# The shared projections as seven half-size products instead of eight, in a gated-DeltaNet and attention trunk

## The chip, the cores and the metric

The kernel runs on one core of a Trainium2 chip. A core has TensorE (PE: matrix products and transposes), VectorE (DVE), ScalarE (ACT), GpSimd (POOL) and SyncE (SP), which here issues the DMAs. The metric is the device time of one launch in microseconds, lower is better.

## The reference

One sequence of 2048 tokens and width 1024 passes a gated-DeltaNet layer and then an attention layer. Between them lie four projections that read the same normed rows; they are what the change concerns:

```python
# h: (2048, 1024), after the DeltaNet layer
u = rms_norm(h, kv_norm)
k, v, f = split(u @ kv_w, [1024, 2048])          # kv_w: (1024, 1024 + 1024 + 8)
k = rms_norm(k.reshape(heads of 128), kv_k_norm)
c = cumsum(log_sigmoid(f + kv_forget_bias))
q, z = split(rms_norm(h, fox_pre_norm) @ fox_w_in, [1024])   # (1024, 2048)
q = rms_norm(q.reshape(heads of 128), fox_q_norm)
# per head: softmax(q k^T / sqrt(128) + c_i - c_j, causal) @ v, times silu(z), @ fox_w_out, rms_norm, + h
```

All of it is float32. The kernel keeps that precision by splitting each operand of a product into a high and a low part in the fast matrix format (the high part is a rounded copy, the low part the difference), and by making three matmuls of each product: high by high, high by low, low by high.

## The kernel before

The span has five stages: the DeltaNet layer (0 to about 1250 us: 128 projection passes by quarters of the tokens, woven with the delta rule), its output projection (to 1397), the shared projections (1400.75 to 2169.73), attention over 8 heads (to about 2690), and the last output projection.

**Shared projections** (`Shared`). Tokens are taken in two halves of 1024. `hprep` loads 128 rows of the DeltaNet layer's result (`ht`), scales them by 1/rms, transposes them by eight 128x128 blocks on TensorE and splits the transposes into `hh` and `hl`; for the first half this runs between the steps of the output projection, for the second after the first half. Then `run(half)` goes through 16 blocks of 256 columns (4 each of k, q, v, z). `wsplit` loads a block's weights (two DMAs of 512 KB), multiplies the norm's gain in and splits them: ACT writes the high part (L818), DVE the low part (L819). For each pair `tp` of token tiles, `mm3` (L130 to L132) is called for 2 tiles x 8 pieces of the contraction, that is 48 matmuls of 256 columns. Over 2 halves, 16 blocks and 4 pairs these are 6144 matmuls. The block with number FORGET carries the 8 forget-gate columns as well, so its 384 matmuls have 264 columns.

`finish` handles a pair after the next pair's products: for k and q, ACT squares and sums each head (L854), DVE scales the sums (L855), POOL takes the power -1/2 (L119), DVE multiplies from PSUM (L860), and TensorE transposes (L866) for the store to `kT_d` and `qT_d`. For v the block is copied, for z it becomes z(1 + tanh(z/2)), and both are stored.

The attention's tile pool is opened before the projections run, so the first head's K, Q and gate loads are queued among the projections' own.

**What sets the order.** The program is written in loops; a scheduler places each engine's instructions from the program's order, the waits and the free buffers. Each engine then executes its own list in order: an instruction that waits holds all behind it.

## Time and profile before

| | |
|---|---|
| median of 3 runs | 2910.54 us (2903.28 to 2915.01) |
| the profiled execution's own time | 2906.28 us |
| its span, first to last instruction | 2904.6 us |
| mean granted TensorE clock | 0.989 |
| PE / DVE / ACT / POOL busy, share of the span | 96% / 59% / 46% / 24% |
| shared projections, first to last matmul | 1400.75 to 2169.73 us |

A busy share is an average over stages with different limits, and TensorE's matmuls are pipelined: the distance from one matmul's start to the next one's is what a matmul costs when they follow each other, while the listed duration is longer. Idle time ahead of an instruction stands in brackets in a timeline, with what ended it.

### The profile page before, as it was taken

What the parts mean: (1) busy time and instruction counts of PE and PEld (TensorE: products, weight loads), DVE (VectorE), ACT (ScalarE), POOL (GpSimd) and SP (SyncE); (2) the same over time, 40 slices, a digit from 0 to 9 for tenths busy, and PEclk for the clock granted to TensorE, in tenths of its full rate; (3) what the DMA queues carried; (4) which work ended last, traced back from release to release, by engine and by line L of the source; (5) the groups of instructions that cost most, each with busy time, mean ns of one, the idle gap of its engine ahead of it and who ended that gap; (6) DMA issues with size and microseconds to landing.
All of it is one profiled execution on the core that took longest, in us unless ns stands there. A gap on an engine that the chain in (4) does not pass through costs nothing.

```text
span 2904.6 us, 50726 instructions
## 1 busy us (share of the span) xinstructions
PE 2795.3 (96%) x18406; PEld 2432.1 (84%) x18406; DVE 1717.4 (59%) x5060; ACT 1337.3 (46%) x3695; POOL 704.2 (24%) x712
## 2 busy tenths in 40 slices
PE   7889999999999999899999999999999999999998
PEld 6677788878887788778999999999998888888787
DVE  6776777777767776644333124332329888888422
ACT  5445544454444444434344223443227677676421
POOL 6544211121111111123211000110004444443322
PEclk9999999999999999999999999999999999999999
DMA  7656444444443443645222323223323323232443
GB/s 234 214 163 192 148 153 136 158 150 130 151 159 118 154 137 108 201 141 164 95 88 88 95 95 113 95 88 95 112 82 101 99 91 98 92 97 75 158 140 109
DMA packets 295505, 371.64 MB, mean 128 GB/s; under 512 B 68443, under 2 KB 216150, under 8 KB 294230
## 3 DMA queue, kind: packets, MB, share of 16 engines
q1 hardware_dynamic: 295088, 368.33, 39.4%
q8 instruction: 145, 2.38, 0.3%
q14 instruction: 106, 0.87, 0.1%
q10 hardware_dynamic: 166, 0.06, 0.0%
HBM read 263.40 MB, written 104.92 MB: 127 GB/s over the span
## 4 chain that ended last, share of the span: by engine, by line
PE 64%; DVE 16%; ACT 3%; issue 3%; DMA 2%; POOL 2%; DVEq 0%; POOLq 0%; ACTq 0%; SPq 0%
DVE acc_q L392 4%; PE pt L1129 4%; PE ppv L130 2%; PE ps L132 2%; PE ppq L130 2%; PE ppv L131 2%; PE ppv L132 2%; PE ppq L131 2%; PE ppq L132 2%; PE ppwf L130 2%; PE ppwf L131 2%; PE ppwf L132 2%; PE ppz L130 2%; PE ppz L131 2%; PE ppz L132 2%
## 5 line engine op out<-in xcount | busy, mean ns | idle before, releaser
L130 PE MATMUL pp_q<-xh_q,wh_q 128*128 128x512 f32 x768 | 325.5, 424 | 1.5 <-ACT acc_q L390 0.8
L132 PE MATMUL pp_q<-xh_q,wl_q 128*128 128x512 f32 x768 | 307.3, 400 | 0.0
L131 PE MATMUL pp_q<-xl_q,wh_q 128*128 128x512 f32 x768 | 305.4, 398 | 0.0
L392 DVE SCALAR_TENSOR_TENSOR acc_q<-cx_q,cols,acc_q 128x512 f32<-128x512 f32 x288 | 227.5, 790 | 12.9 <-ACT acc_q L390 9.7
L125 DVE TENSOR_TENSOR pl<-pt,ph 128x512 fp32r<-128x512 f32 (+1 forms) x320 | 192.1, 606 | 37.8 <-ACT ph L124 36.1
L124 ACT CAST ph<-pt 128x512 fp32r<-128x512 f32 (+1 forms) x320 | 161.7, 519 | 89.1 <-PE pt L1129 88.6
L395 ACT ACTIVATE th_q<-acc_q 128x512 f32<-128x512 f32 x96 | 60.8, 633 | 277.5 <-DVE acc_q L392 274.1
L1115 ACT ACTIVATE s<-s,nm 128x128 f32<-128x128 f32 (+15 forms) x128 | 154.5, 1207 | 68.3 <-DVE nm L1113 68.0
L1129 PE MATMUL pt<-ident,s 128*128 128x128 f32 x1088 | 172.1, 273 | 3.4 <-DVE pl L125 2.6
L132 PEld LDWEIGHTS pp_q<-xh_q,wl_q 128*128 128x128 f32 x768 | 145.6, 190 | 34.0
L130 PEld LDWEIGHTS pp_q<-xh_q,wh_q 128*128 128x128 f32 x768 | 146.1, 190 | 27.3 <-ACT acc_q L390 1.3
L131 PEld LDWEIGHTS pp_q<-xl_q,wh_q 128*128 128x128 f32 x768 | 146.0, 190 | 26.3 <-DVE xl_q L240 0.8
L1129 PEld LDWEIGHTS pt<-ident,s 128*128 128x128 f32 x1088 | 133.5, 140 | 33.6 <-DVE pl L125 3.7
L130 PE MATMUL ppk<-wh_k,hh 128*128 128x256 f32 x512 | 146.9, 287 | 2.6 <-issue 2.6
L130 PE MATMUL ppq<-wh_q,hh 128*128 128x256 f32 x512 | 146.8, 287 | 0.0
L130 PE MATMUL ppv<-wh_v,hh 128*128 128x256 f32 (+1 forms) x512 | 144.9, 283 | 0.0
L130 PE MATMUL ppz<-wh_z,hh 128*128 128x256 f32 x512 | 144.3, 282 | 0.0
L132 PE MATMUL ppv<-wh_v,hl 128*128 128x256 f32 (+1 forms) x512 | 143.9, 281 | 0.0
L131 PE MATMUL ppk<-wl_k,hh 128*128 128x256 f32 x512 | 143.9, 281 | 0.0
L131 PE MATMUL ppv<-wl_v,hh 128*128 128x256 f32 (+1 forms) x512 | 143.9, 281 | 0.0
L132 PE MATMUL ppk<-wh_k,hl 128*128 128x256 f32 x512 | 143.8, 281 | 0.0
L131 PE MATMUL ppq<-wl_q,hh 128*128 128x256 f32 x512 | 143.7, 281 | 0.0
(482 smaller groups left out, 8571.7 us busy)
## 6 DMA issues: line engine op xcount, KB each, us to landing
wh_q<-w_d SPq DMA_DIRECT2D x72, 512.0 KB, 3.5
wl_q<-w_d SPq DMA_DIRECT2D x72, 512.0 KB, 4.8
w_d<-wh_q SPq DMA_DIRECT2D x24, 512.0 KB, 4.4
w_d<-wl_q SPq DMA_DIRECT2D x24, 512.0 KB, 3.1
wh_q_z<-w_d SPq DMA_DIRECT2D x24, 512.0 KB, 3.3
wl_q_z<-w_d SPq DMA_DIRECT2D x24, 512.0 KB, 4.1
wr_q<-in_gdn_w_in_dram SPq DMA_DIRECT2D x22, 512.0 KB, 5.2
x_q<-in_x_dram SPq DMA_DIRECT2D x16, 512.0 KB, 4.5
```

The lines of the kernel that those rows point to most:

```text
L124: i = k.nc.scalar.copy(hi, src)
L125: (eng or k.nc.vector).tensor_tensor(out=lo, in0=src, in1=f(hi), op=ALU.subtract)
L130: nc.tensor.matmul(out, ah, bh, start=start, stop=False)
L131: nc.tensor.matmul(out, ah, bl, start=False, stop=False)
L132: nc.tensor.matmul(out, al, bh, start=False, stop=stop)
L392: nc.vector.scalar_tensor_tensor(out=acc, in0=cx[:, j:j + TB], scalar=cw[j], in1=acc, op0=ALU.mult, op1=ALU.add)
L395: nc.scalar.activation(th, acc, AF.Tanh, scale=0.5)
L1115: e = nc.scalar.activation(s[:, 0:w], s[:, 0:w], AF.Exp, bias=nm, accum_out=ls[:, ii:ii + 1])
L1129: nc.tensor.transpose(out=pt[:, ii * P:(ii + 1) * P], in_=Ps[ii][:, j * P:(j + 1) * P], identity=k.ident)
```

## The change

The product of 256 token rows by 512 columns over 1024 of contraction, which was 2 x 2 x 2 block products, becomes the Winograd form of Strassen's product: seven block products of (128 rows) x (512 of contraction) x (256 columns), of row sums and column sums.

- **Rows.** `prep` makes, for a pair of token tiles, the four quarters of the transposed rows, three further sums of them on POOL (four subtractions or additions of 128x512) and splits all seven operands. The row operands of three pairs at most are kept (`BLOCKS` of 2, 3 and 3 pairs).
- **Weights.** The gain is multiplied into all four 1024x1024 weights during the DeltaNet layer (`gain`: 32 times a load of 512 KB, a 128x1024 ACT instruction and a store of 512 KB to `wg_d`). For each of 24 groups (3 blocks of pairs x 8 groups of 512 columns, in the order k, k, q, q, v, v, z, z) `raw` loads 2 x 1 MB, `sums` makes four differences of 128x1024 on POOL, and `columns` splits the seven column operands (ACT the high part, DVE the low part, 128x1024 each).
- **Products.** Per group, product and pair 12 matmuls of 256 columns: 24 groups hold 64 pair-groups, 64 x 7 x 12 = 5376 matmuls.
- **Results.** A product is added up in PSUM with others where the form allows it and then taken out: two ACT copies and five DVE additions of 128x256 per pair-group.
- **k and q.** `finish` works on the 256x512 result in SBUF: ACT squares 128x1024, DVE sums per head (`tensor_reduce`), POOL takes the power (128x8), DVE multiplies 128x1024 with the result, and eight transposes follow on TensorE 5 and 6 ticks later (a tick is one pair of one product).
- **Forget gate.** `forget` makes 32 matmuls of 128 columns per pair and two small transposes.
- **Attention's pool** is opened after the projections have closed theirs.

```diff
+    def gain():
+        count[0] += 1
+        if count[0] % 3 or not gained:
+            return
+        i, kt = gained.pop(0)
+        wn, base, col = (("kv_w", 0, C_KVN), ("fox_w_in", 0, C_FPN), ("kv_w", D, C_KVN), ("fox_w_in", D, C_FPN))[i]
+        w = ins[wn] if wn == "kv_w" else ins[wn][0]
+        wr = p2.tile([P, D], F32, tag="x", bufs=4, name=f"wgr{i}_{kt}")
+        nc.sync.dma_start(wr, w[kt * P:(kt + 1) * P, base:base + D])
+        nc.scalar.activation(wr, wr, AF.Copy, scale=k.cols[:, col + kt:col + kt + 1])
+        nc.sync.dma_start(wg_d[i, kt], wr)
...
+        s1 = p2.tile([P, 4, P], F32, tag="s1", name=f"s1_{p}")
+        both(s1, q[1, 0], q[1, 1], ALU.add)
+        parts(q[0, 0], "P1")
+        yield
+        both(q[1, 0], q[0, 0], q[1, 0], ALU.subtract)
+        both(q[0, 0], s1, q[0, 0], ALU.subtract)
+        parts(q[0, 0], "P6")
...
+        for i, terms in enumerate(((("P1", 0), ("P2", 4)), (("P5", 0), ("P4", 8)))):
+            for j, (name, w0) in enumerate(terms):
+                for kt in range(4):
+                    for n, part in enumerate(self.rows[name, slot]):
+                        nc.tensor.matmul(pf[:, i], self.wf[:, w0 + kt], part[:, kt], start=i + j + kt + n == 0,
...
+    def sums(self, g, i):
+
+        lo, hi = self.quads[g, 0], self.quads[g, 1]
+        T = self.quads
+        a, b = {1: (lo[:, :, 1], lo[:, :, 0]), 2: (hi[:, :, 1], T.get((g, "T1"))), 3: (hi[:, :, 1], lo[:, :, 1]),
+                4: (hi[:, :, 0], T.get((g, "T2")))}[i]
+        t = T[g, f"T{i}"] = T[g, "T2"] if i == 4 else self.tt.tile([P, 4, 256], F32, tag=f"T{i}", name=f"T{g}_{i}")
+        self.k.nc.gpsimd.tensor_tensor(out=t, in0=a, in1=b, op=ALU.subtract)
...
+        self.raw(0)
+        for i in (1, 2, 3):
+            self.sums(0, i)
+        for n in range(ahead):
+            ready.append(self.columns(*work[n]))
...
+            if pi == 0:
+                cc, one, X, Y = {}, {}, {}, {}
+                if g + 1 < NG:
+                    self.raw(g + 1)
+                self.sums(g, 4)
+            if g + 1 < NG and pi in (2, 4, 5):
+                self.sums(g + 1, {2: 1, 4: 2, 5: 3}[pi])
+            if n + ahead < len(work):
+                ready.append(self.columns(*work[n + ahead]))
+            bh, bl = ready.pop(0)
...
+                    for j, (a, w) in enumerate(((ah, bh), (ah, bl), (al, bh))):
+                        nc.tensor.matmul(R, a[:, kt], w[:, kt], start=first and kt + j == 0,
+                                         stop=last and kt + j == 5, skip_group_check=True)
...
+                if name != "P1":
+                    c = cc[p]
+                    c11, c12, c21, c22 = (c[:, i, j * 256:j * 256 + 256] for i in range(2) for j in range(2))
...
+                    nc.scalar.copy(one[p], R)
+                elif name == "P2":
+                    nc.scalar.copy(c11, R)
...
+                    dst, src = {"P6": (c12, one[p]), "P7": (c21, c12), "P5": (c22, c21), "P4": (c21, c12), "P3": (c12, c12)}[name]
+                    nc.vector.tensor_tensor(out=dst, in0=src, in1=R, op=ALU.add)
+                if name == "P3":
+                    self.finish(g, p, c, pend)
+                tick()
...
+            sq = self.q1.tile([P, 8, P], F32, tag="sq", name="sq" + n)
+            nc.scalar.activation(sq, c8, AF.Square)
+            ss = q2.tile([P, 8], F32, tag="kss", name="kss" + n)
+            nc.vector.tensor_reduce(out=ss, in_=sq, axis=mybir.AxisListType.X, op=ALU.add)
+            nc.vector.tensor_scalar(out=ss, in0=ss, scalar1=1.0 / P, scalar2=EPS, op0=ALU.mult, op1=ALU.add)
+            rs = q2.tile([P, 8], F32, tag="krs", name="krs" + n)
+            rsqrt(k, rs, ss, 8)
+            nc.vector.tensor_tensor(out=c8, in0=c8, in1=rs.unsqueeze(2).to_broadcast([P, 8, P]), op=ALU.mult)
...
+                for i in range(4):
+                    h, t = i // 2, i % 2
+                    nc.tensor.transpose(out=pt[:, i], in_=c8[:, 4 * t + 2 * hh + h], identity=k.ident)
...
+            pend.append([5, lambda: turn(0)])
+            pend.append([6, lambda: turn(1)])
...
-    at = Attention(k, ar)
...
+    sh.run(h_d)
     sb.close()
     sa.close()
+    at = Attention(k, ar)
```

(In the first lines of `run`, `PRODUCTS` is the order P1, P6, P7, P5, P2, P4, P3, and operands are split two products ahead.)

**Order on VectorE in a k column block, before.** `kssk`, `knk` and `ppk` carry block and pair in their names; `wl` is the low part of the next block's weights. L860 reads PSUM.

```order
L860 TENSOR_SCALAR knk2_0_16200<-ppk2_0_16063,krsk2_0_16198 128x128 x4
L819 SCALAR_TENSOR_TENSOR wl_k3_0_16360<-wr_k3_0_1_16371,cols_87,wh_k3_0_16359 128x256 x4
L855 TENSOR_SCALAR kssk2_1_16260<-kssk2_1_16260 128x4
L860 TENSOR_SCALAR knk2_1_16272<-ppk2_1_16139,krsk2_1_16270 128x128 x4
L855 TENSOR_SCALAR kssk2_2_16336<-kssk2_2_16336 128x4
L860 TENSOR_SCALAR knk2_2_16348<-ppk2_2_16211,krsk2_2_16346 128x128 x4
L855 TENSOR_SCALAR kssk2_3_16430<-kssk2_3_16430 128x4
L860 TENSOR_SCALAR knk2_3_16442<-ppk2_3_16287,krsk2_3_16440 128x128 x4
```

The four scalings of a pair follow its own sums, and its transposes come after the next pair's products.

**Order on VectorE after, where a q group (10, pairs 2 to 4) ends and a v group (11) begins.** `gl11_P7` is the low part of a column operand of group 11, `cc10_2` the 256x512 result of pair 2, `kss` its sums and `krs` their power; L989 takes a product out of PSUM.

```order
L1037 TENSOR_REDUCE kss10_2_19143<-sq10_2_19141 128x8
L989 TENSOR_TENSOR cc10_4_18921<-cc10_4_18921,Y10_4_18977 128x256
L1038 TENSOR_SCALAR kss10_2_19143<-kss10_2_19143 128x8
L125 TENSOR_TENSOR gl11_P7_19197<-T11_3_19079,gh11_P7_19196 128x1024
L1041 TENSOR_TENSOR cc10_2_18861<-cc10_2_18861,krs10_2_19146 128x1024
L1037 TENSOR_REDUCE kss10_3_19164<-sq10_3_19162 128x8
L1038 TENSOR_SCALAR kss10_3_19164<-kss10_3_19164 128x8
L1041 TENSOR_TENSOR cc10_3_18891<-cc10_3_18891,krs10_3_19167 128x1024
L1037 TENSOR_REDUCE kss10_4_19185<-sq10_4_19183 128x8
L989 TENSOR_TENSOR cc11_2_19257<-one11_2_19201,X11_2_19200 128x256
L1038 TENSOR_SCALAR kss10_4_19185<-kss10_4_19185 128x8
L125 TENSOR_TENSOR gl11_P5_19254<-T11_1_18943,gh11_P5_19253 128x1024
```

Sums, power and product of three pairs now follow one another in one list with the splits of the next group's operands between them.

**Order on GpSimd at the same place, after.** `T11_2` to `T12_2` are the differences of weights for groups 11 and 12; before, this engine held only the powers here.

```order
L913 TENSOR_TENSOR T11_2_19034<-w11_1_18797,T11_2_19034 128x1024
L119 TENSOR_TENSOR krs10_2_19146<-kss10_2_19143,mhalf_76 128x8
L913 TENSOR_TENSOR T12_3_19475<-w12_1_19193,w12_0_19191 128x1024
L119 TENSOR_TENSOR krs10_3_19167<-kss10_3_19164,mhalf_76 128x8
L119 TENSOR_TENSOR krs10_4_19188<-kss10_4_19185,mhalf_76 128x8
L913 TENSOR_TENSOR T12_1_19339<-w12_0_19191 128x1024
L913 TENSOR_TENSOR T12_2_19430<-w12_1_19193,T12_1_19339 128x1024
```

A power (L119) now stands behind a difference of weights, and between two powers stands another.

**Order on SyncE before, where the projections end.** `vtz` are blocks of z, `kr`, `qr`, `vr` and `zr` loads for attention with the head's number.

```order
L889 DMA z_d_105<-vtz3_5_24425 128x2x256
L889 DMA z_d_105<-vtz3_6_24479 128x2x256
L889 DMA z_d_105<-vtz3_7_24484 128x2x256
L1006 DMA vr0_0_24679<-v_d_104 128x4x128
L1025 DMA qr0_3_24711<-qT_d_103 128x512
L1138 DMA zr0_0_24824<-z_d_105 128x4x128
L1138 DMA zr0_1_24860<-z_d_105 128x4x128
L1006 DMA vr0_1_24858<-v_d_104 128x4x128
L1004 DMA kr1_0_24874<-kT_d_102 128x512
```

Of head 0 only the last quarter of Q, V and z stand behind the last store; the other K and Q loads come earlier in the list.

**Order on SyncE after, at the same place.** `cc23` are the last three results of z.

```order
L1064 DMA z_d_106<-cc23_5_23955 128x2x512
L1064 DMA z_d_106<-cc23_6_23969 128x2x512
L1064 DMA z_d_106<-cc23_7_23983 128x2x512
L1187 DMA kr0_0_24254<-kT_d_103 128x512
L1187 DMA kr0_1_24260<-kT_d_103 128x512
L1187 DMA kr0_2_24266<-kT_d_103 128x512
L1187 DMA kr0_3_24272<-kT_d_103 128x512
L1321 DMA zr0_0_24562<-z_d_106 128x4x128
L1321 DMA zr0_1_24598<-z_d_106 128x4x128
L1208 DMA qr0_0_24278<-qT_d_104 128x512
L1208 DMA qr0_1_24297<-qT_d_104 128x512
```

All K and Q loads of head 0 now stand behind the last stores of z.

## Rows read from the trace of the kernel before

**Rows 1.** Busy by stretch: length, PE, PEld, DVE, ACT, POOL, granted clock, DMA share, GB/s.
```profile
300.00:1200.00 900.00, 876.47 (x5641) 717.19 (x5641) 657.41 (x2190) 426.71 (x1378) 135.72 (x112) 1.00 0.45 145
1200.00:1300.00 100.00, 87.76 (x515) 71.27 (x514) 53.93 (x161) 36.33 (x103) 29.93 (x30) 0.93 0.45 137
1400.00:1500.00 100.00, 98.75 (x833) 98.22 (x834) 35.20 (x114) 41.78 (x177) 18.38 (x18) 1.00 0.29 94
1900.00:2000.00 100.00, 100.00 (x851) 100.00 (x850) 32.22 (x107) 39.89 (x165) 15.12 (x15) 1.00 0.28 89
```

**Rows 2.** Groups of instructions on TensorE, 1400 to 2170 us.
```profile
L130 PE MATMUL ppk<-wh_k,hh 128*128 128x256 f32 x512 | 146.9, 287 | 2.6 <-issue 2.6
L130 PE MATMUL ppv<-wh_v,hh 128*128 128x264 f32 x128 | 36.3, 284 | 0.0
L866 PE MATMUL ptrk<-ident,knk 128*128 128x128 f32 x128 | 20.2, 276 | 0.5 <-DVE knk L860 0.5
```

**Rows 3.** Timeline of TensorE where the projections end: start, duration, instruction.
```profile
2165.84 0.28 PE L130 MATMUL ppz<-wh_z,hh 128*128 128x256 f32 x1
...
2169.73 0.22 PE L130 MATMUL ps<-kh,qh 128*128 128x128 f32 x1
2169.79 0.28 PE L131 MATMUL ps<-kl,qh 128*128 128x128 f32 x1
2169.90 0.27 PE L132 MATMUL ps<-kh,ql 128*128 128x128 f32 x1
2170.01 0.33 PE L130 MATMUL ps<-kh,qh 128*128 128x256 f32 x1
```

**Rows 4.** Timeline of TensorE where the projections begin.
```profile
1397.14 1.04 PE L790 MATMUL pth<-ident,ht 128*128 128x128 f32 x8
1400.75 0.36 PE L130 MATMUL ppk<-wh_k,hh 128*128 128x256 f32 x1 [2.58 <-issue]
```

**Rows 5.** Groups of instructions on VectorE, whole span.
```profile
L125 DVE TENSOR_TENSOR olwg<-orwg,ohwg 128x1024 fp32r<-128x1024 f32 x16 | 19.6, 1223 | 7.4 <-ACT ohwg L124 7.4
L785 DVE TENSOR_SCALAR ht<-ht,hrs 128x1024 f32<-128x1024 f32 x16 | 13.1, 818 | 19.1 <-DMA ht<-h_d 19.1
L437 DVE TENSOR_TENSOR attn_q0g<-pk_q,E_q 128x256 f32<-128x256 f32 x16 | 6.7, 417 | 0.0
```

**Rows 6.** Groups of instructions on GpSimd, whole span.
```profile
L119 POOL TENSOR_TENSOR rn_q<-ssn_q,mhalf 128x8 f32<-128x8 f32 x32 | 52.9, 1653 | 278.2 <-DVE ssn_q L417 275.8 <-DMA d_q0g<-Ti_q0g 2.1
L125 POOL TENSOR_TENSOR vl<-vr,vh 128x512 fp32r<-128x512 f32 x32 | 41.5, 1296 | 82.3 <-ACT vh L124 81.8
L1035 POOL TENSOR_TENSOR cd<-cb 128x1024 f32<-128x1024 f32 x7 | 13.3, 1896 | 39.2 <-DVE mx L1106 39.2
```

**Rows 7.** Groups of instructions on ScalarE, whole span.
```profile
L124 ACT CAST ohwg<-orwg 128x1024 fp32r<-128x1024 f32 x16 | 16.8, 1048 | 7.9 <-PE ppwg L131 7.9
L212 ACT ACTIVATE jx_q<-x_q 128x1024 bf16<-128x1024 f32 x16 | 16.9, 1057 | 8.4 <-DMA x_q<-in_x_dram 8.2
```

**Rows 8.** Timeline of VectorE, early in the projections and in attention.
```profile
1404.15 1.27 DVE L819 SCALAR_TENSOR_TENSOR wl_k<-wr_k,cols,wh_k 128x256 fp32r<-128x256 f32 x3
...
2223.95 0.69 DVE L125 TENSOR_TENSOR kl<-kr,kh 128x512 fp32r<-128x512 f32 x1
2225.37 2.43 DVE L125 TENSOR_TENSOR ql<-qr,qh 128x512 fp32r<-128x512 f32 x1
```

**Rows 9.** Timeline of GpSimd at the same places.
```profile
1400.02 2.52 POOL L722 TENSOR_TENSOR ywg<-ywg,xrwg 128x512 f32<-128x512 f32 x2 [0.92 <-DVE ywg L719]
1404.31 0.72 POOL L119 TENSOR_TENSOR hrs<-s1wg,mhalf 128x1 f32<-128x1 f32 x1 [1.77 <-DVE s1wg L729]
...
2223.99 3.25 POOL L1035 TENSOR_TENSOR cd<-cb 128x1536 f32<-128x1536 f32 x1
```

**Rows 10.** DMA issues: tensor, count, KB each, us to landing.
```profile
kr<-kT_d SPq DMA_DIRECT2D x32, 256.0 KB, 3.0
cb<-c_d SPq DMA_DIRECT2D x8, 1024.0 KB, 5.5
```

More of the change, by code (lines that the diff above doesn't have):

```diff
@@ L191, in gdn @@
     kept = []
+    gained = [(i, kt) for i in range(4) for kt in range(KT)]
+    count = [0]
+    def gain():
[9 more added lines that the diff above has]
+        nc.sync.dma_start(wg_d[i, kt], wr)
     turns, first = [], {}
@@ L313, in wsplit @@
                 nc.sync.dma_start(f(wl), w_d[ct, 1])
+                gain()
                 return wh, wl
@@ L795, in hprep, with parts @@
                 yield
-        self.hT[tb] = (hh, hl)
-    KINDS = (("k", "kv_w", 0, C_KVN), ("q", "fox_w_in", 0, C_FPN), ("v", "kv_w", D, C_KVN), ("z", "fox_w_in", D, C_FPN))
-    def wsplit(self, i, half):
+        pool = self.a2 if slot == 2 else self.a1
+        def parts(src, name):
+            hi = pool.tile([P, 4, P], F32R, tag=f"h{name}_{slot}", name=f"h{name}_{p}")
+            lo = pool.tile([P, 4, P], F32R, tag=f"l{name}_{slot}", name=f"l{name}_{p}")
+            split(k, hi, lo, src)
+            self.rows[name, slot] = hi, lo
@@ new lines, in both @@
+        def both(out, a, b, op):
+            nc.gpsimd.tensor_tensor(out=out, in0=a, in1=b, op=op)
+        s1 = p2.tile([P, 4, P], F32, tag="s1", name=f"s1_{p}")
[5 more added lines that the diff above has]
+        parts(q[0, 0], "P6")
+        yield
+        parts(q[1, 0], "P7")
+        yield
+        parts(s1, "P5")
+        yield
+        parts(q[0, 1], "P2")
@@ L802, in wsplit, with forget_weights @@
+        yield
+        parts(q[1, 1], "P4")
+        yield
+        both(q[0, 1], q[0, 1], q[0, 0], ALU.subtract)
+        parts(q[0, 1], "P3")
+        yield
+    def forget_weights(self):
         k = self.k
         nc = k.nc
-        kind, wn, base, gcol = self.KINDS[i // 4]
-        w = self.ins[wn] if wn == "kv_w" else self.ins[wn][0]
-        col = base + (i % 4) * 256
-        nm = f"{kind}{i % 4}_{half}"
-        pool = (self.p1, self.q1)[i % 2] if i else self.p1
-        n = 256 + (H if i == FORGET else 0)
@@ new lines, in forget_weights @@
+        for kt in range(KT):
+            nc.vector.tensor_scalar(out=wr[:, kt], in0=wr[:, kt], scalar1=k.cols[:, C_KVN + kt:C_KVN + kt + 1],
+                                    scalar2=None, op0=ALU.mult)
+        nc.vector.tensor_tensor(out=wr[:, KT:12], in0=wr[:, 4:KT], in1=wr[:, 0:4], op=ALU.subtract)
+        nc.scalar.copy(self.wf[:, :, 0:H], wr)
+        nc.vector.tensor_tensor(out=self.wf[:, :, H:2 * H], in0=wr, in1=f(self.wf[:, :, 0:H]), op=ALU.subtract)
+        self.t = self.q1.tile([P, L // P, H], F32, name="ft")
@@ L824, in run @@
+    def run(self, h_d):
         k, q2 = self.k, self.q2
         nc = k.nc
[L826 to L898 removed]
@@ L899, in run, with tick @@
-        last[0](*last[1:])
+        NG = 8 * len(self.BLOCKS)
+        work = [(g, name) for g in range(NG) for name in PRODUCTS]
+        ready = []
+        ahead = 2
+        pend = []
+        def tick():
+            for e in list(pend):
+                e[0] -= 1
+                if e[0] < 0:
+                    pend.remove(e)
+                    e[1]()
+        self.raw(0)
[3 more added lines that the diff above has]
+            ready.append(self.columns(*work[n]))
@@ L1234, in tile_yoco @@
     chain.close()
-    sh = Shared(k, ins, dram, sa)
-    halves = (x for tb in range(2) for x in sh.hprep(tb, h_d))
-    ready = [2 * KT * (i + H_LAG) + j * KT for i in range(8) for j in range(2)]
+    sh = Shared(k, ins, dram, wg_d, sa)
+    parts = (x for p, slot in sh.BLOCKS[0] for x in sh.prep(p, slot, h_d))
+    ready = [2 * KT * (i + H_LAG) + j * KT for i in range(4) for j in range(2)]
+    ready = ready[0:4] + [ready[3] + 8 + 2 * i for i in range(7)] + ready[4:8] + [ready[7] + 8 + 2 * i for i in range(7)]
     for _ in steps:
@@ L1242, in tile_yoco @@
             ready.pop(0)
-            next(halves)
-    for _ in halves:
+            next(parts)
+    for _ in parts:
         pass
-    first = sh.wsplit(0, 0)
     wo.close()
-    at = Attention(k, ar)
     sh.open2(sb)
-    sh.run(0, first)
-    first = sh.wsplit(0, 1)
-    for tb in (2, 3):
-        for _ in sh.hprep(tb, h_d):
-            pass
-    sh.run(1, first)
+    sh.run(h_d)
     sb.close()
     sa.close()
+    at = Attention(k, ar)
     w2 = []
```

276 lines of the change are left out of this document (163 added, 113 removed).

## The prediction, made before the changed kernel ran

> **What bounds the kernel now.** I read the busy shares of the span first, then the stretches, then TensorE's timeline at both ends of the shared projections, and last the durations of the operations that the change uses more of. In the stretches [rows 1] the reader is to see that TensorE is occupied 98.75 and 100 of 100 us in the projections at a granted clock of 1.00, while VectorE is at 32 to 35, ScalarE at 40 to 42 and GpSimd at 15 to 18. So this stage is bound by matmuls. A matmul of 256 columns costs its distance to the next: 33 from 2165.84 to 2169.73 are 0.118 us each; one of 128 columns costs 0.11 (2169.79 to 2169.90 to 2170.01) [rows 3]. The stage lasts 769.0 us, from 1400.75 [rows 4] to 2169.73 [rows 3]. Its content is 6144 x 0.118 = 725.0 (twelve groups of 512 and the like [rows 2]), 1.4 for eight more columns in 384 of them (0.118 x 8/256 each), and 256 + 64 transposes at 0.11 = 35.2, together 761.6. The other 7.4 us are waits.
>
> **What goes and what comes on TensorE.** 768 matmuls go: -90.6, and the eight columns: -1.4. The forget gate comes back as 256 matmuls of 128 columns: +28.2. (They are small, but TensorE pays almost as much for 128 columns as for 256.) The 256 transposes of k and q stay; 32 transposes of rows move from the output projection, where TensorE is just as full, into this stage: nothing. So the work falls by 63.8, and since I count the new kernel's waits one by one, I take off the old 7.4 too: -71.
>
> **What the other engines get.** Per group seven low parts of 128x1024 on VectorE, 1.22 each [rows 5]: 8.5 us; five additions of 128x256 from PSUM per pair, 0.42 each [rows 5]; for k and q a sum and a product of 128x1024 per pair. The product has two SBUF inputs like the low part: 1.2. The sum has no like in the trace: between 0.82 (one-input operation of that size) and 1.22 [rows 5]; I take 1.1, since it must read each element and accumulate. On GpSimd four differences of 128x1024 per group: between 1.90 and 2 x 1.30 = 2.6 [rows 6]; I take 2.4, nearer to the two-input subtraction. With three pairs a group has 252 matmuls or 29.7 us, with two pairs 19.8. VectorE needs 8.5 + 6.3 + 6.9 = 21.7 in a k or q group of three pairs, GpSimd 9.6 + 3 x 1.65 = 14.6. By sums it fits. Two things make it not fit by order.
>
> First, the two engines exclude each other. VectorE's low part of 128x512, from SBUF, takes 0.69 at 2223.95; at 2225.37 the same operation takes 2.43, and ends at 2227.80, 0.56 after GpSimd's 128x1536 that began at 2223.99 and ran 3.25 [rows 8, 9]. So it waited for all of it. The Trainium skill (SBUF — State Buffer, Who interferes with whom) says that a VectorE instruction with two SBUF inputs and a GpSimd instruction that reads SBUF take a shared port in turn, and whichever comes first keeps it; the trace agrees with the 2.43. By that rule GpSimd's power would hold the port as well. The row does not bear this out for a short one: at 1404.31 a power of 0.72 runs beside three low parts that take 1.27 together, as they do alone [rows 8, 9]. By the rule 32 powers of 1.65 would delay operand splits by up to 53 us of VectorE, most of it where VectorE waits for them anyway; the sum below has none of it.
>
> Second, the end of a k or q group is a chain. In its order above, VectorE's list is sum, (split), product, sum, product, sum, split, product, so each pair's power on GpSimd lies between two VectorE instructions of which the later one blocks the next pair: sum 1.1 + power 1.65 [rows 6] + product 1.2 + two or three handovers of some 0.1 = 4.2 us per pair. TensorE comes for a pair every 12 matmuls and 8 transposes, 1.4 + 0.9 = 2.3 us.
>
> **Step through a three-pair group,** from the end of the first pair's last product. Addition 0.4, ACT's square 1.06 [rows 7], sum 1.1, scaling 0.1, handovers: the power starts at 3.2 and ends at 4.85. Then GpSimd starts the next difference at once and holds it to 7.3; the product waits for it and ends at 8.5 to 9. TensorE wants the transposes after five pair-products, 5 x 12 x 0.118 = 7.1. The second pair: sum, then its power, product done at about 13, wanted at 11.3 with the first delay counted; the third, behind an operand split, at 17 to 20, wanted at 15.6 to 16.4. Together 3.7 to 7.4, I take 5.3. Eight such groups: +42 (28 to 59). With two pairs the power stands behind a difference of 2.4; the product ends at 9.6, wanted at 6.85: 2.75 in each of four groups, +11 (8 to 14).
>
> **The row operands** of six pairs are made during groups of products: seven splits of 128x512 at 0.69 and four GpSimd operations at 1.30 are 10 us that exclude each other. A v or z group of three pairs has 29.7 - 8.5 - 9.6 = 11 us free of this, one of two pairs 2 us. Pairs 3 and 4 fall into groups of two pairs: I take +14 there and +6 for the others, +20 (0 to 40).
>
> **The start.** Now TensorE waits 2.58 between the last transposes and the first product [rows 4]. After the change the second half of the first weights is queued on SyncE behind the last rows of the output projection, which end at 1400.02 + 2.52 = 1402.5 on GpSimd [rows 9]. A store's issue and a load of 1 MB (5.5 [rows 10]) bring it to 1408.5; then the second difference, 2.4, and the split, 1.05 [rows 7] + 1.22. The second product starts at about 1413 and only 2 x 12 matmuls (2.8) lie ahead of it: +11 (8 to 16).
>
> **The end.** The first attention matmul now comes 0.12 behind the last one of z [rows 3], because head 0's K and Q were loaded earlier. In the new order they stand behind the last stores of z, which wait for the addition, the tanh and the product: 0.4 + 1.06 + 1.2; then a load lands in 3.0 [rows 10], and a cast (half of 1.05) and a split (0.69 [rows 8]) follow: 6.9. Ahead of the first Q are three stores of 512 KB and six loads of 256 KB, 3 MB in all: nothing if they overlap what waits, 16 us if they went one by one at 1 MB in 5.5 [rows 10]. I take 3: +10 (7 to 23).
>
> **The DeltaNet stage** gets 32 loads, ScalarE instructions of 1.06 and stores. TensorE is occupied 876 of 900 us there, DMA 0.45, ScalarE 427 [rows 1]. There is room for 34 us of ScalarE; but each instruction waits for a load issued just before it and holds the convolution's scalings behind it. I take +6; if each cost its own time it would be 34, so 0 to 35.
>
> **The clock.** In the stretch where TensorE is occupied 87.8 of 100 us the granted clock is 0.93, in the full ones 1.00 [rows 1]. The k and q groups would be 4 x 24.5 + 8 x 37.5 = 398 us at about 87%; if they fell alike, 398 x 0.87 x 0.06 = 21. Short gaps spread evenly may not do that: I take +5 (0 to 21).
>
> **The sum:** -71 + 42 + 11 + 20 + 11 + 10 + 6 + 5 = +34. On the profiled execution's 2906.3 that is 2940; the median of the runs is 4.2 above it, which I leave within the range. What this measurement can tell from no change is about 0.5%, 14.5 us, so 2925 and 2896 are the bounds.
>
> **Rivals.**
> A. The forecast, 2905 to 2970, chance 0.46.
> B. Some half of the waits: the differences of weights finish before the powers are due (GpSimd at 1.9 instead of 2.4) and the lower ends hold. Three-pair groups 24, two-pair groups 6, rows 8, ends 18, rest 4: +60 against -71, 2895. For it: by sums VectorE and GpSimd are free a third of the time. Against: the chain of 4.2 against 2.3 needs no GpSimd difference. Chance 0.20.
> C. The saving arrives: the products wait for nothing but the two ends (+21) and some 8 us: -42, 2864. For it: TensorE alone bounded the stage, and the transposes are put 5 and 6 pair-products late, so the first pair is nearly covered. Against: second and third pair. Chance 0.21, faster.
> D. Worse: the clock falls to 0.93 in k and q groups (21 instead of 5), the DeltaNet stage pays for each gain instruction (34 instead of 6): 2984. For it: the stretch at 87.8. Against: the load has a queue of its own in time, and ScalarE is half idle. Chance 0.13.
>
> Slower by over 0.5%: 0.41 of A and all of D, 0.54. Within 0.5%: 0.05 of A, 0.12 of B, 0.01 of C: 0.18. Faster: 0.08 of B and 0.20 of C: 0.28. The range reaches down into C and up to D: 2866 to 2986; the forecast's own is 2905 to 2970.
>
> **What would show it.** TensorE's timeline at the end of a k or q group: idle ahead of the transposes (L1049), released by VectorE's product (L1041), 2 to 3 us per pair with three pairs, or none (C). VectorE's L125 and L1041 with mean durations over 1.22 and a maximum near 2.4 to 3.6 show the exclusion; means of 1.2 refute it. The second product of the first group should start near 1413. The first attention matmul should be about 10 us behind the last product. The stretch 300 to 1200 should be longer by some us, or not. I am wrong above all if the products' own waits in the twelve v and z groups are larger than the chain, or if the chain is hidden.

## The result and the profile after

The changed kernel takes 3066.65 us (median of 4 runs, 3062.26 to 3070.30) against 2906.91 (4 runs); the ratio is 1.0546 (95% interval 1.0515 to 1.0577). The direction is the one forecast; the loss, some 160 us, is nearly five times the 34 forecast and lies outside the range. The profiled execution took 3070.3 us with a span of 3068.3 and a mean granted clock of 0.957.

The same stretches of time as in [rows 1], with two of the projections, columns as there:

```profile
300.00:1200.00 900.00, 868.46 (x5616) 709.95 (x5607) 648.34 (x2160) 449.74 (x1394) 134.95 (x112) 0.99 0.55 178
1200.00:1300.00 100.00, 92.89 (x534) 74.96 (x533) 55.34 (x174) 37.61 (x108) 25.79 (x26) 0.93 0.46 135
1700.00:1800.00 100.00, 87.51 (x646) 85.70 (x645) 52.24 (x71) 32.35 (x44) 31.20 (x14) 0.86 0.21 69
2200.00:2300.00 100.00, 98.17 (x809) 98.03 (x810) 56.53 (x104) 36.15 (x49) 24.38 (x11) 0.97 0.28 99
```

In 1700 to 1800 (k and q groups of three pairs) TensorE is occupied 87.5 of 100 us at a clock of 0.86, in 2200 to 2300 (mostly v and z groups) 98.2 at 0.97. The stage is not slow everywhere. Its ends, as in [rows 3, 4]:

```profile
1413.87 0.39 PE L132 MATMUL ppwg<-wgwh,olwg 128*128 128x512 f32 x1
1421.24 0.77 PE L978 MATMUL X<-gh_P,hP 128*128 128x256 f32 x2 [6.55 <-POOL hrs L119]
```

```profile
2316.99 0.28 PE L978 MATMUL Y<-gh_P,lP 128*128 128x256 f32 x1
2334.92 0.44 PE L130 MATMUL ps<-kh,qh 128*128 128x128 f32 x1 [17.65 <-ACT qh L124]
```

The last matmul of the output projection starts at 1413.87 instead of 1396.90 (+17.0), the last one of the projections 903.1 us later instead of 772.7 (+130.4), and the first one of attention 17.9 after that instead of 0.1 (+17.8). What follows is 1.5 shorter. Together 163.7, the whole difference of the spans.

Inside the stage, summed over TensorE's timeline from the first product to the last (895.7 us): 702 are the work at the distances of [rows 3], as worked out; 120 are idle time, 75 of it ahead of the transposes of k and q (L1049); 73 are matmuls at a wider distance. By groups, the twelve in which a finish of k or q falls (from the second k group of a block to its first v group) carry 140 of these 193 us, the very first group 13, the other eleven 41. One group's waits:

```profile
1799.80 0.28 PE L978 MATMUL Y<-gh_P,lP 128*128 128x256 f32 x1
...
1810.35 0.89 PE L1049 MATMUL ptr<-ident,cc 128*128 128x128 f32 x4 [3.18 <-DVE cc L1041]
1810.89 0.56 PE L978 MATMUL X<-gh_P,hP 128*128 128x256 f32 x1
1811.26 0.41 PE L978 MATMUL X<-gl_P,hP 128*128 128x256 f32 x1
...
1814.66 0.63 PE L1049 MATMUL ptr<-ident,cc 128*128 128x128 f32 x4 [0.26 <-DVE cc L1041]
...
1817.81 0.28 PE L978 MATMUL X<-gl_P,hP 128*128 128x256 f32 x1
1822.20 1.09 PE L1049 MATMUL ptr<-ident,cc 128*128 128x128 f32 x4 [4.12 <-DVE cc L1041]
```

The matmul at 1799.80 is the last of the first pair's products. Ahead of this pair's transposes TensorE waits 3.18 us for L1041, the product with the power; after that matmuls follow each other at 0.21 instead of 0.118 until the second pair's transposes begin; ahead of the third pair's it waits 4.12. Waits (7.6) and wider distances (4.6) together make the group 44.5 us long, where its work is 32.3. From 1822 to 1827 the granted clock is 0.50, which is the level of 1.2 GHz, and from 1830 on it is 1.00:

```profile
1822.00:1827.00 5.00, 4.80 (x23) 4.83 (x24) 2.03 (x4) 2.21 (x3) 0.00 (x0) 0.50 0.05 18
1830.00:1845.00 15.00, 15.00 (x129) 15.00 (x128) 7.02 (x11) 5.21 (x7) 2.41 (x1) 1.00 0.35 112
```

What VectorE and GpSimd do ahead of the first and the last of these waits:

```profile
1802.56 1.22 DVE L1037 TENSOR_REDUCE kss<-sq 128x8 f32<-128x1024 f32 x1 [0.61 <-ACT sq L1035]
1804.03 0.17 DVE L1038 TENSOR_SCALAR kss<-kss 128x8 f32<-128x8 f32 x1
1804.10 1.22 DVE L125 TENSOR_TENSOR gl_P<-T,gh_P 128x1024 fp32r<-128x1024 f32 x1
1806.85 3.36 DVE L1041 TENSOR_TENSOR cc<-cc,krs 128x1024 f32<-128x1024 f32 x1 [1.53 <-POOL krs L119]
...
1813.29 1.23 DVE L1041 TENSOR_TENSOR cc<-cc,krs 128x1024 f32<-128x1024 f32 x1 [1.75 <-POOL krs L119]
...
1815.96 1.22 DVE L125 TENSOR_TENSOR gl_P<-T,gh_P 128x1024 fp32r<-128x1024 f32 x1
1818.70 3.35 DVE L1041 TENSOR_TENSOR cc<-cc,krs 128x1024 f32<-128x1024 f32 x1 [1.53 <-POOL krs L119]
```

```profile
1801.12 2.41 POOL L913 TENSOR_TENSOR T<-w,T 128x1024 f32<-128x1024 f32 x1 [10.33 <-DVE gl_P L125]
1804.27 2.54 POOL L119 TENSOR_TENSOR krs<-kss,mhalf 128x8 f32<-128x8 f32 x1 [0.74 <-DVE kss L1038]
1806.78 2.34 POOL L913 TENSOR_TENSOR T<-w,w 128x1024 f32<-128x1024 f32 x1
...
1816.19 2.48 POOL L119 TENSOR_TENSOR krs<-kss,mhalf 128x8 f32<-128x8 f32 x1 [2.94 <-DVE kss L1038]
1818.64 2.34 POOL L913 TENSOR_TENSOR T<-w 128x1024 f32<-128x1024 f32 x1
```

The power is issued at 1804.27, 0.17 behind a split on VectorE (1804.10 to 1805.32), and takes 2.54 instead of 1.65 [rows 6]: it waits for the split. It ends at 1806.81; the next difference of weights has started on GpSimd at 1806.78, and the product, issued at 1806.85, takes 3.36 instead of 1.2: it waits for the difference. So the exclusion works in both directions within one chain, and the third pair's chain repeats it (2.48 and 3.35); the second pair has neither a split ahead of its power nor a difference behind it, and its product takes 1.23. Over all groups (columns as in [rows 5, 6]):

```profile
L1041 DVE TENSOR_TENSOR cc<-cc,krs 128x1024 f32<-128x1024 f32 x32 | 77.6, 2424 | 61.6 <-POOL krs L119 61.6
L125 DVE TENSOR_TENSOR gl_P<-T,gh_P 128x1024 fp32r<-128x1024 f32 x96 | 125.8, 1311 | 45.1 <-ACT gh_P L124 45.1
L1037 DVE TENSOR_REDUCE kss<-sq 128x8 f32<-128x1024 f32 x32 | 38.8, 1213 | 4.1 <-ACT sq L1035 4.0
```

```profile
L913 POOL TENSOR_TENSOR T<-w,T 128x1024 f32<-128x1024 f32 x48 | 115.1, 2399 | 390.8 <-DVE gl_P L125 380.6 <-DVE f L894 9.8 <-DMA w<-wg_d 0.4
L913 POOL TENSOR_TENSOR T<-w,w 128x1024 f32<-128x1024 f32 x24 | 61.1, 2545 | 29.6 <-DVE gl_P L125 21.4 <-DVE kss L1038 6.1 <-DMA w<-wg_d 2.1
L913 POOL TENSOR_TENSOR T<-w 128x1024 f32<-128x1024 f32 x24 | 59.2, 2466 | 29.1 <-DVE gl_P L125 21.9 <-DVE kss L1038 7.2
L119 POOL TENSOR_TENSOR krs<-kss,mhalf 128x8 f32<-128x8 f32 x32 | 68.0, 2126 | 52.5 <-DVE kss L1038 52.5
```

The 32 powers and the 32 products by shortest, median and longest, in ns:

```profile
L119 POOL TENSOR_TENSOR krs<-kss,mhalf x32: 1630/2476/2551, 1460.0 to 2195.9; 128x8 f32<-128x8 f32 x32
L1041 DVE TENSOR_TENSOR cc<-cc,krs x32: 1224/3352/3366, 1461.7 to 2198.1; 128x1024 f32<-128x1024 f32 x32
```

The means, 2.42 for the product and 2.13 for the power, mix two kinds: 18 products take 3.35 to 3.37 and the other 14 the plain 1.22 to 1.23, and the 18 belong to the same pairs as the 18 powers that take over 2. The sum per head (1.21), the differences (2.40 to 2.55) and the splits (1.31) are near what I had sized (1.1, 2.4, 1.22).

### The profile page after: what moved, and what is told of

Read it like the earlier page. It is cut to its first block, busy times and chain, and to the rows that moved or that the text cites. A ratio compares the mean times of both kernels' runs of the same rounds, so it can differ in the third digit from the quotient of the medians.

```text
span 3068.3 us, 49714 instructions
## 1 busy us (share of the span) xinstructions
PE 2810.4 (92%) x17910; PEld 2434.8 (79%) x17910; DVE 2051.3 (67%) x5094; ACT 1448.2 (47%) x3288; POOL 991.8 (32%) x810
## 4 chain that ended last, share of the span: by engine, by line
PE 52%; DVE 20%; POOL 5%; issue 5%; ACT 4%; DMA 3%; SPq 0%; DVEq 0%; POOLq 0%; ACTq 0%
PE Y L978 9%; PE X L978 5%; DVE acc_q L409 4%; PE pt L1312 3%; POOL krs L119 2%; DVE cc L1041 2%; PE ps L132 2%; PE ppwf L132 2%; PE ppwf L130 2%; PE ppwf L131 2%; PE ps L130 2%; PE ps L131 2%; PE po L132 2%; PE po L131 2%; PE po L130 2%
## 5 line engine op out<-in xcount | busy, mean ns | idle before, releaser
L978 PE MATMUL Y<-gh_P,hP 128*128 128x256 f32 x1024 | 302.4, 295 | 14.3 <-DVE cc L989 11.3
L978 PE MATMUL Y<-gl_P,hP 128*128 128x256 f32 x1024 | 299.0, 292 | 0.0
L978 PE MATMUL Y<-gh_P,lP 128*128 128x256 f32 x1024 | 297.5, 291 | 0.0
L978 PE MATMUL X<-gh_P,hP 128*128 128x256 f32 x768 | 229.1, 299 | 19.8 <-POOL hrs L119 6.5
L978 PE MATMUL X<-gl_P,hP 128*128 128x256 f32 x768 | 225.2, 293 | 8.9 <-DVE gl_P L125 8.9
L978 PE MATMUL X<-gh_P,lP 128*128 128x256 f32 x768 | 225.8, 294 | 2.1 <-DVE lP L125 2.1
L978 PEld LDWEIGHTS Y<-gh_P,hP 128*128 128x128 f32 x1024 | 206.8, 202 | 16.7 <-issue 9.3
L978 PEld LDWEIGHTS Y<-gl_P,hP 128*128 128x128 f32 x1024 | 204.8, 200 | 0.0
L978 PEld LDWEIGHTS Y<-gh_P,lP 128*128 128x128 f32 x1024 | 204.5, 200 | 0.0
L989 DVE TENSOR_TENSOR cc<-cc,Y 128x256 f32<-128x256 f32 x256 | 104.9, 417 | 103.2 <-PE Y L978 102.7
L978 PEld LDWEIGHTS X<-gh_P,hP 128*128 128x128 f32 x768 | 155.9, 203 | 21.2 <-ACT gh_P L124 7.5
```

The costliest lines, as they stand in the source:

```text
L978: nc.tensor.matmul(R, a[:, kt], w[:, kt], start=first and kt + j == 0, stop=last and kt + j == 5, skip_group_check=True)
L989: nc.vector.tensor_tensor(out=dst, in0=src, in1=R, op=ALU.add)
```

## The experiments

The table gives the median, the kernel before in the same runs, the ratio with its interval, and TensorE's time per group: q of three pairs (the second one of block 1) and q of two pairs (the second one of block 0); in either falls the finish of the q group before it. The groups' times are worked out from TensorE's timeline, from one group's first product to the next one's; the work alone would be 32.3 and 21.6.

| kernel | us | before | ratio | q, 3 pairs | q, 2 pairs |
|---|---|---|---|---|---|
| changed kernel | 3066.65 | 2906.91 | 1.0546 (1.0515 to 1.0577) | 44.5 | 30.2 |
| e1 gain step alone | 2924.98 | 2911.96 | 1.0037 (1.0022 to 1.0052) | | |
| e2 attention's pool late | 2923.29 | 2911.96 | 1.0039 (1.0026 to 1.0052) | | |
| e3 waits filled | 3070.54 | 2911.96 | 1.0534 (1.0517 to 1.0552) | 43.1 | 28.5 |
| e4 later transposes | 3070.77 | 2911.96 | 1.0531 (1.0512 to 1.0550) | 43.4 | 30.7 |
| e5 no differences | 2962.91 | 2908.36 | 1.0183 (1.0165 to 1.0201) | 37.9 | 24.2 |
| e6 no normalising | 2945.91 | 2908.36 | 1.0118 (1.0098 to 1.0137) | 32.6 | 22.3 |
| e7 differences on VectorE | 2982.13 | 2908.36 | 1.0245 (1.0228 to 1.0262) | 37.6 | 24.8 |
| e8 staged finish | 3040.76 | 2908.36 | 1.0443 (1.0426 to 1.0460) | 40.3 | 29.2 |
| e9 e7, e8, e10 together | 2926.83 | 2908.05 | 1.0067 (1.0046 to 1.0088) | 32.3 | 22.8 |
| e10 gain step, loads ahead | 2917.24 | 2908.05 | 1.0030 (1.0018 to 1.0042) | | |
| e11 e9, gain in the groups | 2968.66 | 2911.31 | 1.0199 (1.0178 to 1.0221) | 35.3 | 28.5 |
| e12 e11, row sums on VectorE | 2949.34 | 2911.31 | 1.0135 (1.0113 to 1.0156) | 35.3 | 28.1 |
| e13 e9, row sums on VectorE | 2908.53 | 2910.80 | 0.9990 (0.9979 to 1.0000) | 32.3 | 21.9 |

Against what was expected: e6, e8, e10 and e13 fall into the range of their theory, e3 into that of its rival and e4 at its upper end. e5, e7 and e9 came out faster than either range, e11 and e12 slower than both. e1 and e2 are near or in their ranges only because the kernel before took 2912 us and not 2907 in these runs: their differences, 13 and 11 us, lie between theory and rival.

**e1, e10: the DeltaNet stage.** e1 adds `gain()` with its call and `wg_d` to the kernel before, as in the diff above; e10 also moves each load ahead:

```diff
+        if loaded:
+            i, kt, col, wr = loaded.pop()
+            nc.scalar.activation(wr, wr, AF.Copy, scale=k.cols[:, col + kt:col + kt + 1])
+            nc.sync.dma_start(wg_d[i, kt], wr)
+        if gained:
...
+            nc.sync.dma_start(wr, w[kt * P:(kt + 1) * P, base:base + D])
+            loaded.append((i, kt, col, wr))
```

> The kernel before, with the gain step added to the DeltaNet stage (32 times load, ScalarE 128x1024, store); what it writes is read by nobody, so the output is unchanged. Theory: the 17 us by which the changed kernel's last matmul of the first output projection is late (1413.87 against 1396.90) come from this step alone, and since the changed kernel has 32 transposes (3.5 us) less there, the step costs about 20: 2925 to 2929 against 2907. Rival: the step costs about the 6 us I had put down and the rest comes from the row preparation in the output projection: 2911 to 2915.

> The kernel before with the gain step, each load issued one step before the ScalarE instruction that needs it. Theory: the 14 us by which the DeltaNet stage became longer come from ScalarE waiting for a load just issued; with the loads ahead half or more goes: 2912 to 2918 against 2908. Rival: they come from the added DMA and ScalarE work itself in three bursts: 2919 to 2925.

The gain step costs 0.37% (0.22 to 0.52), 11 to 13 us in the timed runs. In the profiled executions the output projection begins at 1173.15 before, at 1187.33 in e1 and at 1186.89 in the changed kernel: what the DeltaNet layer loses is this step's. The output projection behind it has a loss of its own. From its first matmul to its last it takes 227.4 us in e9 and 219.4 in e13, which moves the row sums to VectorE; e11 and e12 part alike (228.5, 219.6). So the row sums on GpSimd cost it some 8 us, hidden in part by the transposes that left it. e10's 0.30% (0.18 to 0.42) does not part from e1's, though its output projection begins 9 us earlier in the one profiled execution (1177.93); whether the wait for the load makes the loss stays open.

**e2: the end.** In the kernel before:

```diff
-    at = Attention(k, ar)
     sh.open2(sb)
...
     sa.close()
+    at = Attention(k, ar)
```

> The kernel before, with attention's tile pool opened after the projections have closed theirs. Theory: the wait of 17.65 us ahead of the first attention matmul comes from the order of the loads alone; here it would be 13 to 18 us and the time 2920 to 2925. Rival: the load order costs some 7 (a load, a cast, a split) and the rest of the 17.65 is the finish of z for three pairs, which this kernel does not have: 2913 to 2916.

```profile
2188.05 0.44 PE L130 MATMUL ps<-kh,qh 128*128 128x128 f32 x1 [15.76 <-ACT qh L124]
```

15.76 us of waiting without Strassen's product: the order of the loads makes the wait at the end, not the finish of z. The runs show 11 us.

**e3, e4: is TensorE's waiting the cost?** e3 puts matmuls into the waits; e4 puts the transposes later.

```diff
+                for _ in range(fill):
+                    nc.tensor.matmul(pt[:, 0:2].rearrange("p a b -> p (a b)"), filler[:, 0],
+                                     filler[:, 0:2].rearrange("p a b -> p (a b)"), start=True, stop=True)
```

```diff
-                    cc[p] = q2.tile([P, 2, 512], F32, tag="cc", bufs=4, name=f"cc{nm}")
+                    cc[p] = q2.tile([P, 2, 512], F32, tag="cc", bufs=6, name=f"cc{nm}")
...
-            pend.append([5, lambda: turn(0)])
-            pend.append([6, lambda: turn(1)])
+            pend.append([12, lambda: turn(0)])
+            pend.append([13, lambda: turn(1)])
```

> The changed kernel with idle matmuls of 256 columns put ahead of the transposes of k and q, where TensorE waits 2 to 4 us: 24 ahead of a group's first pair, 30 (with two pairs 16) ahead of its last; their results are overwritten. 592 matmuls, 70 us of work at 0.118, in the place of 71 us of idle time. Theory: the granted clock falls because of these waits, and what follows each runs at 0.21 instead of 0.118 per matmul; with the waits filled the clock stays up there and the kernel gets faster although it does more: 3020 to 3040 against 3067. Rival: the clock is low for another reason (the mean load of the stage), or the waits simply move behind the added work: 3067 to 3110.

> The changed kernel with the transposes of k and q 12 and 13 ticks after a pair's last product instead of 5 and 6, and six buffers for the results instead of four (the buffers of the row preparation go from two to one to make room). Theory: the chain sum, power, product of 4.2 us per pair is long but not a throughput bound; with the transposes later the 71 us of waits ahead of them go, and the slow stretches behind them (about 40 us): 2950 to 2975. Rival: VectorE and GpSimd exclude each other so much that they bound these groups, and the waits return ahead of products or additions: 3030 to 3070.

The theories of both fell. In e3 the clock did rise: 0.97 in the stretch that had 0.86.

```profile
1700.00:1800.00 100.00, 88.21 (x728) 86.49 (x727) 49.20 (x68) 31.04 (x43) 29.00 (x14) 0.97 0.20 66
```

Yet the group takes 43.1, against 44.5. The waits ahead of the transposes did not vanish: of 75 us 40 are left, behind matmuls worth 70. The groups with the forget gate became 3 to 4 us longer, and the timed runs show no gain: TensorE was waiting for something with a pace of its own. In e4 the waits ahead of the transposes went, and one of 8 us came ahead of a product:

```profile
1824.40 0.55 PE L978 MATMUL Y<-gh_P,hP 128*128 128x256 f32 x1 [8.03 <-DVE cc L989]
```

It waits for additions (L989) of the next group, which stand in VectorE's list behind the whole chain. The chain on VectorE, not TensorE's place in it, sets these groups.

**e5, e6, e7: which part of the chain?** e5 leaves the differences out, e6 the normalising (the results of both are not the reference's), e7 does the differences on VectorE:

```diff
-        t = T[g, f"T{i}"] = T[g, "T2"] if i == 4 else self.tt.tile([P, 4, 256], F32, tag=f"T{i}", name=f"T{g}_{i}")
-        self.k.nc.gpsimd.tensor_tensor(out=t, in0=a, in1=b, op=ALU.subtract)
+        T[g, f"T{i}"] = a
```

```diff
-            sq = self.q1.tile([P, 8, P], F32, tag="sq", name="sq" + n)
...
-            nc.vector.tensor_tensor(out=c8, in0=c8, in1=rs.unsqueeze(2).to_broadcast([P, 8, P]), op=ALU.mult)
```

```diff
-        self.k.nc.gpsimd.tensor_tensor(out=t, in0=a, in1=b, op=ALU.subtract)
+        self.k.nc.vector.tensor_tensor(out=t, in0=a, in1=b, op=ALU.subtract)
```

> The changed kernel without the 96 differences of weights on GpSimd; the raw quarters take their place, so the results are not the reference's, and everything else is done. Theory: GpSimd's 128x1024 differences hold VectorE's products by 2.1 us twice in each three-pair k or q group, and stand ahead of powers and operand splits elsewhere; with them gone the first and last waits of a group fall from 3.2 and 4.2 to 1 to 2, and the slow matmuls behind them with them: 2985 to 3010 against 3067. Rival: the chain of sum, power, product in VectorE's list costs its time without any exclusion: 3040 to 3067.

> The changed kernel without square, sum, power and product of k and q (their rows are not normalised; transposes and stores stay). Theory: this chain on VectorE and GpSimd makes all waits at the ends of the k and q groups: 71 us of idle time and some 45 us of matmuls at half rate go: 2945 to 2965. Rival: without the chain VectorE and GpSimd still hold the groups by splits and differences, or the clock stays down: 3000 to 3050.

> The changed kernel with the differences of weights on VectorE instead of GpSimd, 4 x 1.2 us more on VectorE per group and nothing of 128x1024 left on GpSimd. Theory: if exclusion is the larger part, the loss of 2.1 us twice per group is worth more than 4.9 us of VectorE that is partly idle: 3010 to 3045. Rival: VectorE's list is the bound in k and q groups, 4.9 us per group come on top: 3080 to 3130.

Without the differences 104 us go, without the normalising 121. The two savings overlap: together they would be more than all waiting and slow matmuls there are. Most of the loss needs both, the chain and the differences beside it: a q group of three pairs takes 37.9 with the chain alone (e5) and 32.6 with the differences alone (e6). e7 confirms it with all work done: 96 operations that cost GpSimd 235 us are moved onto the engine that already sets the pace, and the kernel gets 85 us faster.

```profile
L1041 DVE TENSOR_TENSOR cc<-cc,krs 128x1024 f32<-128x1024 f32 x32 | 39.2, 1226 | 44.1 <-POOL krs L119 44.1
L913 DVE TENSOR_TENSOR T<-w,T 128x1024 f32<-128x1024 f32 x48 | 58.5, 1219 | 4.0 <-DMA w<-wg_d 3.9
L119 POOL TENSOR_TENSOR krs<-kss,mhalf 128x8 f32<-128x8 f32 x32 | 68.0, 2124 | 375.1 <-DVE kss L1038 375.1
```

The product is back at 1.23, the difference costs VectorE 1.22. The power still takes 2.12 beside the splits, so its own delay is no part of the 85 us. What e5 has more than e7 (19 us) is the price of the differences on VectorE.

A rival to the exclusion is GpSimd's list: a power that stands behind a difference there has to wait for it, and e7 takes that away too. In the changed kernel's trace 21 of the 24 powers of three-pair groups start within 0.14 us of the end of their scaling (L1038), so there the list holds next to nothing, and the exclusion is left as the cause. Of the eight powers of two-pair groups four start 2.35 to 2.93 late, behind a difference; how much of the 5.4 us that e7 takes off such a group belongs to either is not shown.

**e8, e9: the order of the chain.** e8 is e4 with the finish in stages; e9 adds e7's edit and e10's.

```diff
+            def power():
...
+                rsqrt(k, rs, ss, 8)
+
+                def scale():
+                    nc.vector.tensor_tensor(out=c8, in0=c8, in1=rs.unsqueeze(2).to_broadcast([P, 8, P]), op=ALU.mult)
+
+                pend.append([6, scale])
+
+            pend.append([1, power])
```

> The kernel with the later transposes and six result buffers, and with the finish of k and q in stages: sums and power one tick after the last addition, the product six ticks after that, so that the second pair's sum stands ahead of the first pair's product in VectorE's list and its power runs meanwhile. Theory: VectorE's waiting for powers (1.5 to 1.75 us, three times in a group) is what makes the chain long; two of the three go, and with the transposes later TensorE waits less: 3010 to 3045. Rival: the exclusion returns what the order saves: 3060 to 3075.

> Both remedies at once: differences of weights on VectorE, the finish of k and q in stages, later transposes, six result buffers; and the loads of the gain step issued one step ahead. Theory: with the exclusion gone, VectorE's list has room for its 27 us in a group of 32 us of TensorE, and the staged order lets it run ahead: three-pair k and q groups fall from 37.5 (differences on VectorE alone) to 34 or 35, two-pair ones from 24.8 to 22 or 23: 2935 to 2960. Rival: the waits return ahead of the products, as they did with the later transposes alone: 2975 to 2990. In either case it stays above the kernel before, since the DeltaNet stage, the start and the end keep their losses.

With the differences on GpSimd, staging takes 30 us off e4. With them on VectorE, e9 is 55 us faster than e7 (2982 to 2927), more than I expected; this includes the later transposes, the six buffers and the earlier gain loads, which were not parted, and 47 of it lie within the stage. In e9 a q group of three pairs takes what its matmuls take, 32.3, and the clock stays up:

```profile
1700.00:1800.00 100.00, 99.82 (x851) 99.46 (x850) 77.47 (x110) 48.56 (x66) 19.51 (x9) 1.00 0.34 111
```

**e11 to e13: what is left.** e11 takes the gain out of the DeltaNet stage and into each group; e12 and e13 put the row sums on VectorE and head 0's first Q load behind its first K load, on e11 and on e9.

```diff
+            for t in range(4):
+                wt = w[:, t].rearrange("p a b -> p (a b)")
+                self.k.nc.scalar.activation(wt, wt, AF.Copy, scale=self.k.cols[:, col + hf * 4 + t:col + hf * 4 + t + 1])
```

```diff
-            nc.gpsimd.tensor_tensor(out=out, in0=a, in1=b, op=op)
+            nc.vector.tensor_tensor(out=out, in0=a, in1=b, op=op)
```

> The combined kernel without the gain step in the DeltaNet stage: each group's weights come from the inputs and ScalarE multiplies the gain in after the load, eight instructions of 128x512 (4.8 us) per group. Theory: the 12 us of the DeltaNet stage come back, the start loses 3 to the gain ahead of the first operands, and ScalarE has room (about 22 us in a three-pair group of 32): 2914 to 2922 against 2927. Rival: ScalarE's casts of column operands come late in the two-pair groups of 20 to 22 us and TensorE waits there: 2927 to 2945.

> The same, with the row sums on VectorE as well (nothing of 128x512 or more left on GpSimd in the projections) and head 0's first Q load and split put directly behind its first K load. Theory: the first groups of the second and third block (36 and 44 us against 32) lose some 4 us each to the exclusion, and attention's first matmul comes 4 us earlier, since its first block needs only the first quarter of K: 2900 to 2912. Rival: VectorE's list is full there and the transfers at the end are bound by bytes: 2914 to 2922.

> The combined kernel (gain step in the DeltaNet stage) with the row sums on VectorE and head 0's first Q load behind its first K load: the two additions that took 19 us off the kernel with the gain in place. Theory: they act alike here, 9 us in the first output projection, 5 in the groups that make row operands, 4 at the end: 2906 to 2912, no difference from the kernel before. Rival: here VectorE is fuller in the output projection, or the gain step hides part of it: 2915 to 2927.

e11 refutes me: two-pair groups go from 22.8 to 28.5, and TensorE's longest waits are now for ScalarE's copies and casts. e12 takes 19 us off it, e13 18 us off e9. By the traces 7 of e13's lie in the output projection, 11 in the stage and 3 at the end, and 5 are lost again in attention. e13's interval ends at 1.0000: it equals the kernel before and does not beat it. Its end:

```profile
2154.61 0.28 PE L984 MATMUL Y<-gh_P,lP 128*128 128x256 f32 x1
2169.31 0.47 PE L130 MATMUL ps<-kh,qh 128*128 128x128 f32 x1 [14.42 <-ACT qh L124]
```

## Why the prediction was right in direction and wrong in size

- **TensorE's work** was sized right: 697.8 forecast, about 702 by the trace; the saving is there.
- **The step that failed is the exclusion and the chain in the k and q groups.** Put at 37.5 us and 24.5 (32.3 + 5.3, 21.6 + 2.75), they took 44.5 and 30.2; the twelve groups lose 140 us in place of 53 and 5 of clock. In the group shown, the three products were to be done 8.5 to 9, 13 and 17 to 20 us behind the end of the first pair's last matmul; they were done 10.1, 14.4 and 22.0 behind it (1800.08). What was missing: the first and the third power are late by 0.9 and 0.8 behind a split, and the third product, like the first, meets a difference (2.1), where I had put only a split. The mechanism had been named, and e6 shows that little else holds these groups: without the chain a q group of three pairs takes 32.6. Its size was wrong.
- **GpSimd's power waits for VectorE.** I had set this aside on one row, a power of 0.72 beside three low parts. I misread it. In the kernel before, of the sixteen powers of this form the shortest takes 0.549, the median 0.551 and the longest 0.727:

```profile
L119 POOL TENSOR_TENSOR hrs<-s1wg,mhalf x16: 549/551/727, 1210.3 to 1404.3; 128x1 f32<-128x1 f32 x16
```

Two stand above 0.56, at 1316.08 and 1404.31, and these are the two that start some 0.15 us behind a low part of 0.47 or 0.48 us on VectorE. So the row showed the delay, small because the operation ahead was short. The Trainium skill's rule (SBUF — State Buffer, Who interferes with whom), that whichever comes first keeps the port, held both ways: 2.54 for the power, 3.36 for the product. Late power and held product go together in 18 pairs of 18; whether the lateness brings the product into the difference, or the order in GpSimd's list would do so alone, is not shown.
- **The chain holds more than the transposes.** I let it delay these alone; e4 shows that it holds the additions of the next group as well, so the waits returned there when the transposes were put later.
- **The clock**, +5 forecast, shows as 73 us of wider distances. I looked for it in the mean load and not after each wait, where it is: 0.50 for some 5 us behind a wait of 4.12. But e3 shows that it is no term of its own: with the clock at 0.97 the group took 43.1 in place of 44.5. It cannot be added to the waits.
- **The end**, +10 forecast, is +17.8. That the late loads make it was right (e2), and so nearly was the term for transfers: head 0's first K lands 6.9 us after its issue, where I had 3.0 and 3. What I had left out is a second load in series. In the changed kernel's trace, SyncE, VectorE and ScalarE:

```profile
2322.59 2.10 SPq L1187 DMA_DIRECT2D kr<-kT_d  x4
...
2331.27 4.62 SPq L1208 DMA_DIRECT2D qr<-qT_d  x3
```

```profile
2320.92 1.22 DVE L1062 SCALAR_TENSOR_TENSOR cc<-th,cc 128x1024 f32<-128x1024 f32 x1 [1.12 <-ACT th L1061]
...
2330.56 1.89 DVE L125 TENSOR_TENSOR kl<-kr,kh 128x512 fp32r<-128x512 f32 x3
...
2334.86 0.69 DVE L125 TENSOR_TENSOR ql<-qr,qh 128x512 fp32r<-128x512 f32 x1 [1.41 <-ACT qh L124]
```

```profile
2329.47 2.62 ACT L124 CAST kh<-kr 128x512 fp32r<-128x512 f32 x4 [8.58 <-DMA kr<-kT_d]
```

The K and Q loads share four buffers, and the four quarters of K fill them: the first Q load is issued at 2331.27, when VectorE has done the first K split. From the end of the last product of z (2322.1) to Q's split 12.7 us pass, where I had 6.5. Putting Q's load behind the first K load (e13) takes 3.4 off the end and no more, since K and Q then land 6.7 and 7.7 us after their issue.
- **The DeltaNet stage**, +6 forecast, is +13.7 at the first matmul of the output projection and +17 at its last, within the bounds given (0 to 35). Rival D had been answered with a load that has a queue of its own; in the traces SyncE issues the gain's loads in one list with all others.
- **The start**, +11 forecast: the wait before the first product is 7.4 in place of 3.9, and the first group takes 32.4 where its matmuls take 19.8. Together 16, the upper bound.
- **The row operands**, +20 forecast (0 to 40), were not measured alone in the changed kernel. The groups without a finish of k or q, the first one left out, lose 41 us together, most of it where rows are prepared; if all of it is theirs, the term was half of what it should have been, and the upper bound held. e13, with the row sums on VectorE, has 11 less in the stage than e9.
- **The rivals.** The one in which the saving arrives failed through the groups above. The form does allow a part of it: in e13, with the differences and row sums off GpSimd and the finish staged, the stage from the last matmul of the output projection to the last product is 20 us shorter than before (752.6 against 772.7), and 5 ahead of it, 15 at the end and 4 in attention eat that. The highest rival, D at 2984, was still 83 too low. Its clock did fall (0.86 in the stretch shown), but e3 shows that this did not make the loss.
